# Folding a gate into two output weights on GpSimd, and turning the two-map outputs one unit later

## The chip, the cores and the metric

The kernel runs on one core of a Trainium2 chip. The metric is device time in microseconds (us) of one execution. The core's engines work side by side and in order, each from its own queue: TensorE (PE, matmuls, with PEld for its weight loads), VectorE (DVE), ScalarE (ACT), GpSimd (POOL), and SyncE (SP), which here only issues DMAs.

## The reference

A transformer block of two layers on 512 tokens of width 1024, in float32. Layer 0 mixes by eight heads of stick-breaking attention and eight of a sparse attention (an index picks 128 keys per query); layer 1 by eight heads of differential attention, the difference of two softmax maps ("two-map heads"). After each mixer comes a gated output product, a residual and a LayerNorm, then a gated feed-forward. What the change touches is the output product and the differential heads:

```python
h = x * (1.0 + sc_m) + sh_m
y = even_mixer(h, ...)          # or odd_mixer; each ends in  o @ w_out
x = layer_norm(ALPHA * x + (1.0 + g_m) * y, ln_mix_g[i], ln_mix_b[i])

# odd_mixer
p = softmax(where(causal, s, -inf)); a = p[:, :, 0] - lam * p[:, :, 1]
o = einsum('bhqs,bshe->bqhe', a, v)
o = rms_norm(o, subln_g) * (1.0 - lambda_init)
```

The gate `1 + g_m` is one number per output column, the same for all tokens. So `gate * (o @ w)` equals `o @ (w * gate)`.

## The kernel before, in words

**Products.** TensorE has no full float32 here: every operand is kept as a high and a low half of a narrower type, and `mm3` (L321 to L323) issues three matmuls for one product: high by high, high by low, low by high. Weights come from memory as 1 MB tiles `raw` (two buffers), loaded by SP. `split_w` (L288 to L300) makes the halves: ACT copies the high one (`wh`, L295), and the low one is a subtraction (`wl`, L299) on an engine taken in turn from a list, in the two-map stage DVE, DVE, GpSimd.

**Output products.** The 1024 rows of `w_out` are taken as two halves, k0 = 0 and k0 = 4. The first half is multiplied by `down_beside` (L577) while the other heads of the layer are still being made, beside them; the second half by `down_last` (L607). In `down_beside`, for each of two column halves h, `rows_w` (L553) loads four 128-row tiles, they are split, and for each of four token blocks b twelve matmuls sum into a PSUM tile `pd`. Then `partial` (L477) brings it into the residual `xa[b]`: it multiplies by the gate row `grow` into a tile `yt` (L479), and adds that to ALPHA times `xa` (L481), or to `xa` as it is (L483) where it is not the first half.

```python
        t = wd("yt")[:, :cs.stop - cs.start]
        dve.tensor_tensor(t, o, grow[:, cs], op=OP.mult)
        if first:
            dve.scalar_tensor_tensor(xa[b][:, cs], xa[b][:, cs], ALPHA, t, op0=OP.mult, op1=OP.add)
```

The gate rows are themselves made during the attention: `mod_side` sums them (`macc`, `ml` L221, `pm` L223) beside the stick-breaking heads.

**Two-map heads.** `diff_heads` (L1060 on) goes over 8 heads of 4 units (128 queries each). `pipeline` (L903) calls four stages at lags counted in units. `one` makes the two score tiles `zq` (L888), their mask and maximum (DVE, L880, `nm`), exponentials and the difference of the maps, `e`. `two`, L2 = 3 units later, transposes `e` on TensorE (`tp`, L895), and ACT copies that out of PSUM (`pt`, L898). `three`, 4 units behind `one`, multiplies by v into `o_df` (L1112); behind the head's last unit DVE, ACT and GpSimd make the norm: `oc` (L1116), `sq`, `st` (L1121 to L1125), a power on GpSimd (L1126, "the pow"), L1127, and `on` (L1129). `four`, 6 units behind, transposes `on` (L1139, into a tile `po`), and makes the halves `o_h` and `o_l` (L1144) that `down_beside` multiplies. Each head's q and k are split by ACT and GpSimd (L1072, tiles wh and wl 128x512).

**What sets the order.** `weave` mixes a main generator (heads) with a fill generator (projections, then `down_beside`) at a fixed ratio of planned costs; a scheduler then orders each engine's queue. Five buffers of 128x512 with the tag "wd" are shared by pt, oc, sq, on, of, the rope's rq and rt, and yt. PSUM has six banks "z" (zq, tp, o_df, the transposes' po) and two "pp" (projections, pd).

Of the kernel before, what the change touches and what calls it, by code (L numbers as in the profile page):

```python
# [12 lines left out]
OP = mybir.AluOpType  # L13
# [3 lines left out]
P = 128  # L17
S = 512
D = 1024
KT = D // P  # L20
EPS = 1e-5
ALPHA = 4.0 ** 0.25
# [9 lines left out]
TAIL2 = 1  # L32
# [4 lines left out]
L2 = 3  # L37
SEGS = [(0, 6), (6, 6), (12, 6), (18, 4)]
HALF = [slice(0, S), slice(S, 2 * S)]
# [8 lines left out]
def hybrid_kernel(ctx, tc, x, c, positions, w_mod, b_mod, w_in_even, w_out_even, w_in_odd,  # L48
# [3 lines left out]
    pe, act, dve, pool, sp = nc.tensor, nc.scalar, nc.vector, nc.gpsimd, nc.sync  # L52
# [8 lines left out]
    def acc(name="pp"):  # L61
        return ps.tile([P, S], F32, tag="pp", name=name, bufs=2)
# [4 lines left out]
    def wd(name, dt=F32):  # L67
        return T("wd", [P, S], dt, 5, name)
# [22 lines left out]
    xa = [cp.tile([P, D], F32, name=f"xa{b}") for b in range(4)]  # L91
# [94 lines left out]
    rows = {}  # L186
# [85 lines left out]
    def beside(main, side, every):  # L272

        for i, cost in enumerate(main):
            if i % every == every - 1:
                next(side, None)
            yield cost
# [197 lines left out]

    def partial(o, b, cs, grow, first):

        t = wd("yt")[:, :cs.stop - cs.start]
        dve.tensor_tensor(t, o, grow[:, cs], op=OP.mult)  # L479
        if first:  # L480
            dve.scalar_tensor_tensor(xa[b][:, cs], xa[b][:, cs], ALPHA, t, op0=OP.mult, op1=OP.add)  # L481
        else:
            dve.tensor_tensor(xa[b][:, cs], xa[b][:, cs], t, op=OP.add)  # L483
# [69 lines left out]
    def rows_w(w, k0, nk, h):  # L553

        t = raw()[:, :nk * S].rearrange("p (k m) -> p k m", m=S)
        sp.dma_start(t, w[P * k0:P * k0 + P * nk, S * h:S * h + S].rearrange("(k p) m -> p k m", p=P))
        return t
# [16 lines left out]
            for b in range(4):  # L574
                partial(os[b], b, HALF[h], grow, first)

    def down_beside(w, k0, ops, grow, first):  # L577

        for h in range(2):
            t = rows_w(w, k0, 4, h)  # L580
            ws = split_k(t[:, 0:2, :]) + split_k(t[:, 2:4, :])
            for b in range(4):
                bs = slice(P * b, P * b + P)
                o = acc("pd")
                for k in range(4):
                    mm3(o, (ops[k][0][:, bs], ops[k][1][:, bs]), ws[k], k == 0, k == 3)
                    yield 0.65
                partial(o, b, HALF[h], grow, first)

    def down_lead(w, k0, ops, lead=4):  # L590

# [78 lines left out]
    t = raw()  # L670
# [127 lines left out]
    oT = [None] * 8  # L798
# [104 lines left out]
    def pipeline(units, stages, tail):  # L903

        st = [{} for _ in units]
        last = max(lag for _, lag in stages)
        for t in range(len(units) + last):
            for f, lag in stages:
                u = t - lag
                if 0 <= u < len(units):  # L910
                    yield f(units[u], st[u])
            if t >= len(units) - 1:
                yield tail
# [74 lines left out]
    rest = beside(even_rest(), topk, 1)  # L988
    got_rows = []
# [6 lines left out]
    mods0 = mods_even()  # L996
    rest = beside(rest, mods0, 4)
# [3 lines left out]


    def even_fill(rest):
        yield from rest
        while not got_rows:
            next(mods0)
        yield from beside(down_beside(w_out_even[0], 0, oT[:4], rows[0, 2], True), mods0, 2)
        drain(mods0)
    rest = even_fill(rest)
    weave(dsa_heads(qd, kd), rest, DSA_FILL)  # L1010
# [51 lines left out]
    def diff_heads(qk):  # L1062
# [82 lines left out]
            oT[h] = (a, b)  # L1145
            return 0.43

        yield from pipeline([(h, i) for h in range(8) for i in range(4)], ((one, 0), (two, L2), (three, L2 + 1), (four, L2 + 3)), TAIL2)

    qk_od = [(r1("q_od"), r1("k_od")) for _ in range(8)]  # L1150

# [8 lines left out]
    oT = [None] * 8  # L1160
# [3 lines left out]
        next(rest)  # L1164
    def odd_fill():
        yield from rest
        while oT[3] is None:
            yield None
        yield from down_beside(w_out_odd[0], 0, oT[:4], rows[1, 2], True)
    rest2 = odd_fill()  # L1170
    low_on(dve, dve, pool)
    weave(diff_heads(qk_od), rest2, DIFF_FILL)
# [109 lines left out]
```

## Time and profile before

| | us |
|---|---|
| three runs | 1330.69, 1331.32, 1336.52 |
| median | 1331.32 |
| the profiled execution | 1333.38 |
| its span, first to last instruction | 1331.3 |
| mean granted clock of TensorE | 0.985 |

Stages by the trace: first products and the sparse heads' index until some 130 us; stick-breaking heads to 230; sparse heads with the first half of w_out_even beside them, 233 to 290; second half and LayerNorm to 340; feed-forward to 690; v of layer 1 to 750; two-map heads to 930, with the first half of w_out_odd beside them from about 880; second half and LayerNorm to 970; feed-forward to the end.

How to read it: the page gives each engine's busy share of the span; the table by stretches gives the same within a window, with the clock that was granted there (1.00 is full speed); the table of waits adds up an engine's idle time by what ended it; a timeline lists instructions with their start, their length, and in brackets the idle time before them. Names are the program's (out<-in). L-numbers are lines of the kernel before unless the text is about the change.

### The profile page before, as it was taken

The page shows a single profiled execution, that of the slowest core. Times are in us where ns is not written, and L with a number is a line of the kernel's source. Part 1 is how long each engine was busy: PE and PEld are TensorE (multiplying, and loading weights), DVE is VectorE, ACT ScalarE, POOL GpSimd, SP SyncE. Part 2 cuts the span into 40 slices and gives each one's busy share as a digit, 9 for nine tenths or more (in the row PEclk, how much of TensorE's full clock was granted, in tenths as well). Part 3 has the DMA queues.
Part 4 walks back from the last instruction along what each step waited for, and adds up shares of the span by engine and source line. Part 5 has one row for each costly group of instructions (what it writes and reads, how often), then busy time and mean ns, then how long its engine had stood idle before and what let it go on. Part 6 is the DMA issues. An engine that isn't in the chain of part 4 may idle for free.

```text
span 1331.3 us, 17597 instructions
## 1 busy us (share of the span) xinstructions
PE 1283.0 (96%) x6707; PEld 1017.8 (76%) x6707; DVE 885.8 (67%) x1605; ACT 498.8 (37%) x889; POOL 246.4 (19%) x173
## 2 busy tenths in 40 slices
PE   6999998999999999999999999898999999999995
PEld 5767676668888888888888866676888888888884
DVE  3789996987866665665694387787786335335358
ACT  2445544554432222222244356565443322322210
POOL 0103223001800000000017244443280000000004
PEclk9999989999999999999999999999999999999998
DMA  9953234342365555555423422215235223233211
GB/s 265 279 174 95 88 112 139 99 126 96 92 219 157 192 169 173 190 172 189 141 68 111 127 64 84 88 52 175 78 97 190 75 100 110 95 96 95 95 64 63
DMA packets 134388, 169.47 MB, mean 127 GB/s; under 512 B 7800, under 2 KB 89120, under 8 KB 134304
## 3 DMA queue, kind: packets, MB, share of 16 engines
q1 hardware_dynamic: 133568, 167.31, 39.9%
q8 instruction: 52, 0.85, 0.3%
q10 hardware_dynamic: 576, 1.02, 0.2%
q14 instruction: 32, 0.26, 0.1%
q0 software_dynamic: 160, 0.03, 0.0%
HBM read 159.95 MB, written 2.10 MB: 122 GB/s over the span
## 4 chain that ended last, share of the span: by engine, by line
PE 49%; issue 26%; DVE 13%; ACT 4%; DMA 3%; POOL 3%; SPq 1%; DVEq 0%; ACTq 0%; POOLq 0%
PE po L321 7%; PE po L322 7%; PE po L323 7%; PE pd L321 4%; PE pd L323 4%; PE pd L322 4%; DMA wm<-in_w_mod_dram 2%; PE pv L321 1%; PE pv L322 1%; PE pv L323 1%; DMA rt<-rq 1%; PE pf L322 1%; PE pf L323 1%; PE pf L321 1%; DVE yt L479 1%
## 5 line engine op out<-in xcount | busy, mean ns | idle before, releaser
L295 ACT ACTIVATE wh<-raw 128x1024 fp32r<-128x1024 f32 x174 | 183.8, 1065 | 499.8 <-PE po L322 268.6
L299 DVE TENSOR_TENSOR wl<-raw,wh 128x1024 fp32r<-128x1024 f32 x169 | 238.3, 1414 | 169.5 <-ACT wh L295 169.3
L321 PE MATMUL po<-hh,wh 128*128 128x512 f32 x848 | 340.9, 402 | 0.4 <-DVE sg L631 0.3
L323 PE MATMUL po<-hh,wl 128*128 128x512 f32 x848 | 333.4, 393 | 0.0
L322 PE MATMUL po<-hl,wh 128*128 128x512 f32 x848 | 333.3, 393 | 0.0
L321 PEld LDWEIGHTS po<-hh,wh 128*128 128x128 f32 x848 | 160.6, 189 | 40.0 <-issue 6.4
L323 PEld LDWEIGHTS po<-hh,wl 128*128 128x128 f32 x848 | 160.8, 190 | 34.1
L322 PEld LDWEIGHTS po<-hl,wh 128*128 128x128 f32 x848 | 160.9, 190 | 30.4
L502 POOL TENSOR_TENSOR lnv<-lnv,mhalf 128x1 f32<-128x1 f32 x16 | 11.6, 723 | 683.7 <-DVE lnv L500 683.5
L322 PE MATMUL pd<-wl,hid_h 128*128 128x512 f32 x352 | 137.2, 390 | 0.0
L323 PE MATMUL pd<-wh,hid_l 128*128 128x512 f32 x352 | 137.0, 389 | 0.0
L321 PE MATMUL pd<-wh,hid_h 128*128 128x512 f32 x352 | 137.0, 390 | 0.0
L212 DVE SCALAR_TENSOR_TENSOR macc<-wm,silu_c,macc 128x512 f32<-128x512 f32 x140 | 108.1, 775 | 6.8 <-DMA wm<-in_w_mod_dram 4.6
L631 DVE TENSOR_TENSOR sg<-sg,po 128x512 f32<-128x512 f32 x40 | 27.5, 686 | 118.3 <-PE po L323 118.3
L321 PEld LDWEIGHTS pd<-wh,hid_h 128*128 128x128 f32 x352 | 66.1, 188 | 14.1 <-issue 0.4
L322 PEld LDWEIGHTS pd<-wl,hid_h 128*128 128x128 f32 x352 | 66.1, 188 | 13.8 <-DVE wl L299 0.3
L323 PEld LDWEIGHTS pd<-wh,hid_l 128*128 128x128 f32 x352 | 66.1, 188 | 13.7
L479 DVE TENSOR_TENSOR yt<-pd,grow 128x512 f32<-128x512 f32 x96 | 64.1, 682 | 10.2 <-PE pd L323 10.1
L321 PE MATMUL pd<-wh,o_h 128*128 128x512 f32 x128 | 57.0, 445 | 0.0
L323 PE MATMUL pd<-wh,o_l 128*128 128x512 f32 x128 | 51.8, 405 | 0.0
L322 PE MATMUL pd<-wl,o_h 128*128 128x512 f32 x128 | 51.4, 401 | 0.3 <-DVE wl L299 0.3
L1094 ACT ACTIVATE e<-e,nm 128x128 f32<-128x128 f32 (+3 forms) x64 | 35.4, 555 | 36.8 <-DVE nm L1093 25.2
(276 smaller groups left out, 2021.4 us busy)
## 6 DMA issues: line engine op xcount, KB each, us to landing
wm<-in_w_mod_dram SPq DMA_DIRECT2D x56, 512.0 KB, 5.0
raw<-in_w_gate_dram SPq DMA_DIRECT2D x22, 1024.0 KB, 5.4
raw<-in_w_up_dram SPq DMA_DIRECT2D x22, 1024.0 KB, 5.4
wm<-in_w_mod_dram SPq DMA_DIRECT2D x80, 256.0 KB, 4.0
raw<-in_w_down_dram SPq DMA_DIRECT2D x16, 1024.0 KB, 5.1
raw<-in_w_in_odd_dram SPq DMA_DIRECT2D x12, 1024.0 KB, 5.2
raw<-in_w_in_even_dram SPq DMA_DIRECT2D x6, 1024.0 KB, 7.7
raw<-in_w_down_dram SPq DMA_DIRECT2D x12, 512.0 KB, 3.3
```

The source lines that it names most:

```text
L212: dve.scalar_tensor_tensor(a, t[:, k, :], silu_c[:, k0 + k:k0 + k + 1], a, op0=OP.mult, op1=OP.add)
L295: act.activation(oh, src, AF.Copy)
L299: e.tensor_tensor(ol, src, oh, op=OP.subtract)
L321: pe.matmul(o, lhsT=ah, rhs=bh, start=start, stop=False, skip_group_check=True)
L322: pe.matmul(o, lhsT=ah, rhs=bl, start=False, stop=False, skip_group_check=True)
L323: pe.matmul(o, lhsT=al, rhs=bh, start=False, stop=stop, skip_group_check=True)
L479: dve.tensor_tensor(t, o, grow[:, cs], op=OP.mult)
L502: norm_done["pow"] = pool.tensor_tensor(y, v[:, 1:2], mhalf[:, 0:1], op=OP.pow).ins
L631: dve.tensor_tensor(g, g, o, op=OP.mult)
L1094: act.activation(es[j], es[j], AF.Exp, scale=-1.0, bias=nm, accum_out=ss[:, j, i:i + 1])
```

## The change

`partial` gets a short form: with `grow` None it adds the PSUM tile straight to `xa`, one DVE operation (for a first half L481, now `xa<-xa,pd`) and no `yt`. Only `down_beside` uses it. In exchange a new function `gated_rows` loads the rows and multiplies them by the gate row in place, two GpSimd operations of 128x1024 (L589) for each of the four tiles, before they are split. The first tile is asked for earlier: in the even layer during the projections, once the gate row exists, in the odd layer before waiting for the fourth head's output; the second tile in the middle of the first one's products. In `diff_heads`, `three` stands 5 units behind `one` where it stood 4, and `four` 7 where it stood 6.

```diff
--- before.py
+++ after.py
@@ -475,6 +475,13 @@
 
     def partial(o, b, cs, grow, first):
 
+        if grow is None:
+            t = xa[b][:, cs]
+            if first:
+                dve.scalar_tensor_tensor(t, t, ALPHA, o, op0=OP.mult, op1=OP.add)
+            else:
+                dve.tensor_tensor(t, t, o, op=OP.add)
+            return
         t = wd("yt")[:, :cs.stop - cs.start]
         dve.tensor_tensor(t, o, grow[:, cs], op=OP.mult)
         if first:
@@ -574,18 +581,29 @@
             for b in range(4):
                 partial(os[b], b, HALF[h], grow, first)
 
-    def down_beside(w, k0, ops, grow, first):
-
+    def gated_rows(w, k0, h, gate):
+
+        t = rows_w(w, k0, 4, h)
+        for k in range(0, 4, 2):
+            v = t[:, k:k + 2, :]
+            pool.tensor_tensor(v, v, gate[:, HALF[h]].unsqueeze(1).to_broadcast([P, 2, S]), op=OP.mult)
+        return t
+
+    def down_beside(w, k0, ops, grow, first, ts=None):
+
+        first_t = ts.pop() if ts else gated_rows(w, k0, 0, grow)
         for h in range(2):
-            t = rows_w(w, k0, 4, h)
+            t = first_t if h == 0 else t1
             ws = split_k(t[:, 0:2, :]) + split_k(t[:, 2:4, :])
             for b in range(4):
                 bs = slice(P * b, P * b + P)
                 o = acc("pd")
+                if (h, b) == (0, 0):
+                    t1 = gated_rows(w, k0, 1, grow)
                 for k in range(4):
                     mm3(o, (ops[k][0][:, bs], ops[k][1][:, bs]), ws[k], k == 0, k == 3)
                     yield 0.65
-                partial(o, b, HALF[h], grow, first)
+                partial(o, b, HALF[h], None, first)
 
     def down_lead(w, k0, ops, lead=4):
 
@@ -1001,10 +1019,14 @@
 
 
     def even_fill(rest):
-        yield from rest
+        ts = []
+        for n, cost in enumerate(rest):
+            if n >= 4 * KT and got_rows and not ts:
+                ts.append(gated_rows(w_out_even[0], 0, 0, rows[0, 2]))
+            yield cost
         while not got_rows:
             next(mods0)
-        yield from beside(down_beside(w_out_even[0], 0, oT[:4], rows[0, 2], True), mods0, 2)
+        yield from beside(down_beside(w_out_even[0], 0, oT[:4], rows[0, 2], True, ts), mods0, 2)
         drain(mods0)
     rest = even_fill(rest)
     weave(dsa_heads(qd, kd), rest, DSA_FILL)
@@ -1145,7 +1167,7 @@
             oT[h] = (a, b)
             return 0.43
 
-        yield from pipeline([(h, i) for h in range(8) for i in range(4)], ((one, 0), (two, L2), (three, L2 + 1), (four, L2 + 3)), TAIL2)
+        yield from pipeline([(h, i) for h in range(8) for i in range(4)], ((one, 0), (two, L2), (three, L2 + 2), (four, L2 + 4)), TAIL2)
 
     qk_od = [(r1("q_od"), r1("k_od")) for _ in range(8)]
 
@@ -1164,9 +1186,10 @@
         next(rest)
     def odd_fill():
         yield from rest
+        ts = [gated_rows(w_out_odd[0], 0, 0, rows[1, 2])]
         while oT[3] is None:
             yield None
-        yield from down_beside(w_out_odd[0], 0, oT[:4], rows[1, 2], True)
+        yield from down_beside(w_out_odd[0], 0, oT[:4], rows[1, 2], True, ts)
     rest2 = odd_fill()
     low_on(dve, dve, pool)
     weave(diff_heads(qk_od), rest2, DIFF_FILL)
```

The diff shifts lines: by 7 behind `partial`, by 18 from the stick-breaking heads on, by 22 in the two-map heads (tp is L913, pt L916, o_df L1134, oc L1138, the pow L1148, on L1151, the transposes L1161, q and k splits L1094).

**TensorE, around the end of the second head.** Before (tp is of the next head's first unit, o_df x4 of this head's last):

```order
L895 MATMUL tp<-ct,e 128x128
L1112 MATMUL o_df<-v_od,pt 128x128 x4
L321 MATMUL po<-hh,wh 128x512
L322 MATMUL po<-hl,wh 128x512
L323 MATMUL po<-hh,wl 128x512
L321 MATMUL po<-hh,wh 128x512
L322 MATMUL po<-hl,wh 128x512
L323 MATMUL po<-hh,wl 128x512
L888 MATMUL zq<-wl,wh 128x128 x6
```

Now:

```order
L913 MATMUL tp<-ct,e 128x128 x2
L321 MATMUL po<-hh,wh 128x512
L322 MATMUL po<-hl,wh 128x512
L323 MATMUL po<-hh,wl 128x512
L1134 MATMUL o_df<-v_od,pt 128x128 x4
L321 MATMUL po<-hh,wh 128x512
L322 MATMUL po<-hl,wh 128x512
L323 MATMUL po<-hh,wl 128x512
L906 MATMUL zq<-wl,wh 128x256 x6
```

The products o_df of the head's last unit stood directly behind the first transposes of the next head. They now stand one unit later, behind the two transposes of its second unit.

**DVE, at one head's norm in the middle of the two-map heads.** Before (`e,nm<-zq` are the masks, 128x128 those of a head's first unit):

```order
L1095 RECIPROCAL rr<-ss 128x1
L1116 TENSOR_SCALAR oc<-o_df 128x512
L1096 TENSOR_SCALAR rr<-rr,ss,lam 128x1
L1097 SCALAR_TENSOR_TENSOR e<-e,rr 128x512
L1121 TENSOR_REDUCE st<-sq 128x4
L880 ISA e,nm<-zq,bias_c 128x128
L880 ISA nm 128x1
L1123 SCALAR_TENSOR_TENSOR st<-st 128x4
L1124 TENSOR_SCALAR st<-st 128x4
L1093 TENSOR_SCALAR nm<-nm 128x1
L880 ISA e,nm<-zq,bias_c 128x128
L880 ISA nm 128x1
```

Now (L898 are the masks, L1138 is oc):

```order
L1117 RECIPROCAL rr<-ss 128x1
L1118 TENSOR_SCALAR rr<-rr,ss,lam 128x1
L1119 SCALAR_TENSOR_TENSOR e<-e,rr 128x128
L1138 TENSOR_SCALAR oc<-o_df 128x512
L898 ISA e,nm<-zq,bias_c 128x256
L898 ISA nm 128x1
L898 ISA e,nm<-zq,bias_c 128x256
L898 ISA nm 128x1
L1115 TENSOR_SCALAR nm<-nm 128x1
L1117 RECIPROCAL rr<-ss 128x1
L1118 TENSOR_SCALAR rr<-rr,ss,lam 128x1
L1119 SCALAR_TENSOR_TENSOR e<-e,rr 128x256
```

The masks of the next head's first unit stood between the sum and the scaling of the norm; now they, and those of the second unit, stand ahead of the sum.

**GpSimd, heads 5 and 6 of the two-map stage.** Now (L1148 is the pow of a norm, L1166 o_l, L464 the rope):

```order
L589 TENSOR_TENSOR raw<-raw,grow 128x1024 x2
L464 TENSOR_TENSOR rq<-rq,cos_t 128x512
L1166 TENSOR_TENSOR o_l<-of,o_h 128x512
L1094 TENSOR_TENSOR wh<-q_od,wh 128x512
L1148 TENSOR_TENSOR st<-st,mhalf 128x4
L464 TENSOR_TENSOR rq<-rq,cos_t 128x512
L1166 TENSOR_TENSOR o_l<-of,o_h 128x512
L299 TENSOR_TENSOR wl<-raw,wh 128x1024
L1094 TENSOR_TENSOR wl<-k_od,wl 128x512
L464 TENSOR_TENSOR rq<-rq,cos_t 128x512
L589 TENSOR_TENSOR raw<-raw,grow 128x1024 x2
L1148 TENSOR_TENSOR st<-st,mhalf 128x4
```

Before, there was no L589, and the other rows followed one another in much the same turn. The first pair is ahead of a rope product and the Q split of head 6, the second directly ahead of a pow, that of head 4's norm. In the stick-breaking stage a pair stands between the first and the second lo (L854, before L836) of head 4, and another at the same place in head 6; SP's order is the same there. In the two-map stage the second load of w_out_odd stands two ropes (eight DMAs) later in SP's queue than before, directly ahead of the third load, and the last rope's DMAs stand behind both; each load waits for a buffer.

## Rows read from the trace of the kernel before

**Rows 1.** Page, part 1: busy time, share of the span and instructions of each engine.
```profile
PE 1283.0 (96%) x6707; PEld 1017.8 (76%) x6707; DVE 885.8 (67%) x1605; ACT 498.8 (37%) x889; POOL 246.4 (19%) x173
```

**Rows 2.** Table by stretches: us, engines' busy time, granted clock, DMA.
```profile
233.00:290.00 57.00, 56.46 (x387) 38.13 (x388) 51.63 (x160) 30.42 (x85) 5.15 (x4) 0.94 0.31 95
...
840.00:844.00 4.00, 4.00 (x15) 3.09 (x16) 2.61 (x17) 2.44 (x9) 1.01 (x1) 0.57 0.14 33
844.00:848.00 4.00, 4.00 (x25) 3.02 (x24) 1.82 (x6) 1.57 (x5) 1.29 (x1) 1.00 0.14 35
880.00:930.00 50.00, 46.05 (x259) 35.57 (x257) 39.99 (x108) 27.59 (x63) 19.32 (x12) 0.99 0.37 124
928.00:932.00 4.00, 3.81 (x13) 3.17 (x14) 1.23 (x2) 3.06 (x6) 1.29 (x1) 0.63 0.01 4
```

**Rows 3.** Table of TensorE's waits, 740 to 980 us: total us, times, longest.
```profile
PE o_df L1112 <- ACT pt L898: 4.2, 4, 1.8
PE po L1139 <- DVE on L1129: 4.0, 3, 2.6
PE zq L888 <- DVE nm L880: 3.5, 3, 2.1
```

**Rows 4.** Timeline, PE, three places: start, length, idle before and releaser in brackets.
```profile
163.91 0.50 PE L223 MATMUL pm<-ml,cst_r 128*128 128x512 f32 x1 [0.55 <-DVE ml L221]
...
840.00 0.74 PE L888 MATMUL zq<-wl,wh 64*128 64x256 f32 x5 [2.08 <-DVE nm L880]
...
928.19 0.63 PE L1139 MATMUL po<-ct,on 128*128 128x128 f32 x4 [2.60 <-DVE on L1129]
```

**Rows 5.** Groups by line and shape, DVE: count | busy us, mean ns | idle before.
```profile
L299 DVE TENSOR_TENSOR wl<-raw,wh 128x1024 fp32r<-128x1024 f32 x169 | 238.3, 1414 | 169.5 <-ACT wh L295 169.3
...
L479 DVE TENSOR_TENSOR yt<-pd,grow 128x512 f32<-128x512 f32 x96 | 64.1, 682 | 10.2 <-PE pd L323 10.1
...
L631 DVE TENSOR_TENSOR sg<-sg,po 128x512 f32<-128x512 f32 x40 | 27.5, 686 | 118.3 <-PE po L323 118.3
...
L481 DVE SCALAR_TENSOR_TENSOR xa<-xa,yt 128x512 f32<-128x512 f32 x32 | 23.6, 759 | 0.2
```

**Rows 6.** Groups by line and shape, POOL.
```profile
L541 POOL TENSOR_TENSOR xa<-xa,lnb 128x1024 f32<-128x1024 f32 x12 | 37.8, 3173 | 0.0
L540 POOL TENSOR_TENSOR xa<-xa,lng 128x1024 f32<-128x1024 f32 x12 | 34.9, 2931 | 0.0
...
L299 POOL TENSOR_TENSOR wl<-raw,wh 128x1024 fp32r<-128x1024 f32 x5 | 12.1, 2423 | 7.2 <-ACT wh L295 4.0 <-issue 3.3
```

**Rows 7.** Timeline, POOL: a lo of head 4, the pow of head 4, the LayerNorm.
```profile
161.05 1.29 POOL L836 TENSOR_TENSOR lo<-l,hi 128x512 fp32r<-128x512 f32 x1 [1.70 <-DVE hi L835]
...
880.09 1.01 POOL L1126 TENSOR_TENSOR st<-st,mhalf 128x4 f32<-128x4 f32 x1 [3.18 <-PE zq L888]
...
969.96 5.76 POOL L540 TENSOR_TENSOR xa<-xa,lng 128x1024 f32<-128x1024 f32 x2
```

**Rows 8.** Timeline, DVE, four places.
```profile
162.88 0.98 DVE L221 TENSOR_TENSOR ml<-macc,mh 128x512 fp32r<-128x512 f32 x1
...
881.13 0.16 DVE L1127 TENSOR_TENSOR st<-st 128x4 f32<-128x4 f32 x1 [1.05 <-POOL st L1126]
...
921.73 1.78 DVE L481 SCALAR_TENSOR_TENSOR xa<-xa,yt 128x512 f32<-128x512 f32 x1
...
970.17 13.31 DVE L299 TENSOR_TENSOR wl<-raw,wh 128x1024 fp32r<-128x1024 f32 x4 [1.44 <-ACT wh L295]
```

**Rows 9.** Timeline, SP: loads of rows of the two output weights.
```profile
153.62 0.38 SPq L556 DMA_DIRECT2D raw<-in_w_out_even_dram  x1
...
855.74 0.37 SPq L556 DMA_DIRECT2D raw<-in_w_out_odd_dram  x1
...
875.84 0.37 SPq L556 DMA_DIRECT2D raw<-in_w_out_odd_dram  x1
```

**Rows 10.** DMA issues: count, KB each, median us to landing.
```profile
raw<-in_w_out_odd_dram SPq DMA_DIRECT2D x4, 1024.0 KB, 5.7
```


## Prediction, on record before the change was run

> **What bounds the kernel now.** I read the busy shares first: TensorE works 1283.0 of 1331.3 us, 96% [rows 1], so only time that its queue loses can be won, and whatever makes it wait is paid in full. Next comes the table by stretches, for the two places where the change works [rows 2]. In the DSA heads (233 to 290 us), where the first half of w_out_even is multiplied, TensorE is busy 56.46 of 57 us: taking DVE work away there gains at most half a microsecond. In the last two-map heads (880 to 930 us), where the first half of w_out_odd is multiplied, it is busy 46.05 of 50, and DVE 39.99. The table of waits for 740 to 980 us says what TensorE waits for in the two-map stage [rows 3]: 4.2 us in four waits of the second product o_df for ACT's copy pt; 4.0 in three waits of the four transposes po for DVE's normalised rows on; 3.5 in three waits of the scores zq, whose bank is free only once DVE has read it (nm). That is 11.7 us. Last I looked at what follows a wait. After the one of 2.08 us at 840.00 [rows 4] the granted clock is 0.57 over 840 to 844 us, and 1.00 in the next four [rows 2], about the lower of its two levels (1.2 against 2.4 GHz): 4 x 0.43 = 1.7 us of work lost. After the 2.60 us at 928.19 [rows 4] it is 0.63 in 928 to 932 [rows 2]: 4 x 0.37 = 1.5 us. So up to 11.7 + 3.2 = 14.9 us are to be had in this stage.
>
> **Part 1: the gate folded into the weights, on DVE.** Sixteen blocks (8 in each product) lose their yt and keep one operation. Before, a block cost 682 + 759 ns; now it is one op of a PSUM tile and an SBUF tile. Its nearest row is the 686 ns addition of a PSUM tile at L631, its upper bound the 759 ns of the old second op [rows 5]. DVE saves 682 to 755 ns a block, 10.9 to 12.1 us in all. I count the even half of it as nothing, since TensorE is full there [rows 2]; if TensorE were not, it would be worth 0.5 us. The odd half (about 6 us out of DVE's 39.99) shortens waits counted in part 3 and is not counted again.
>
> **Part 2: the same fold, on GpSimd.** Eight operations are added, each 128x1024 with two SBUF inputs. The rows of that shape on GpSimd are 2423, 2931 and 3173 ns [rows 6]; I take 2.93, so 23.4 us (19.4 to 25.4), and a pair is 5.9 us. GpSimd is idle most of the time, so the cost is in what queues behind a pair, and in DVE. At 969.96 us GpSimd runs two of its 128x1024 multiplications in 5.76 us, with more such work behind them [rows 7], and the four splits wl on DVE beside them take 13.31 us [rows 8], 3.33 each against a mean of 1.41 over the run [rows 5]: a DVE op with two SBUF inputs is held for about the length of a GpSimd op.
> The Trainium skill (GPSIMD Engine Reference, 1. Specifications) says the same, that GpSimd shares its SBUF interfaces with VectorE and contends with instructions that have two SBUF inputs; these rows agree, and by it the fold would lengthen DVE's queue rather than relieve it.
>
> *Even, first pair.* The load goes out at 153.62 [rows 9] and, at the 5.7 us that the other product's loads take [rows 10], lands at 159.3. In the built order the pair stands between the first and the second lo of head 4, so it runs at about 159.4 to 165.3 (the first lo is done by then) and pushes the second lo from 161.05 [rows 7] to 165.3. I find no wait of TensorE on lo in this stage, and count that as nothing; without that cover it would cost the same 4 us. But DVE's ml, 0.98 us at 162.88 [rows 8], has two SBUF inputs, and TensorE already waits 0.55 us for it at 163.91 [rows 4]. Held by one gate operation it ends 2.4 us later, held by both 4.9 us; by none, it costs 0. I take 1.5, as the ml may just as well fall between the two. The second pair lies in head 6 with no such wait nearby: 0.
>
> *Odd, first pair.* It stands behind the K split of head 5 and ahead of a rope multiply and the Q split of head 6. A score of head 6 needs that split. From 0, if the ropes' lead covers it, to a whole pair, 5.9; I take 2.0: TensorE has about a dozen projection products to do before it needs those scores, an estimated 2 to 3 us (259 matmuls take 46.05 us in 880 to 930 [rows 2], 0.18 each, the wide ones more), and the rope's DMAs leave some room too.
>
> *Odd, second pair.* Its load waits for a buffer that GpSimd's own split frees, and the pair stands directly ahead of the pow of head 4 (before at 880.09 [rows 7]). DVE's next operation, at 881.13, already waits 1.05 us for that pow [rows 8] with masks and partials queued behind it in order, and TensorE needs those masks to get score banks back. 0 if the rows land well ahead of the pow; 5.9 if the pair starts when the pow is due. I take 2.0, nearer the low end, because the built order gives TensorE a dozen projection products between chain and transposes. In SP's queue the third load and the last rope's DMAs stand behind this load, so its wait can hold head 7's k as well; that is the same lateness seen from another queue, with a head of some 20 us in between, and I add nothing for it beyond the 5.9.
>
> Each pair also holds one of the two raw buffers 5.9 us longer and the next load into it starts that much later. Loads land in 5.7 us (median) [rows 10] and go out 20 us apart (855.74, 875.84 [rows 9]): 0. With less lead it would be another 5.9.
>
> **Part 3: the later turn.** o_df now comes one unit (about 5 us: 32 units in the 160 us from 770 to 930) later, behind its neighbour's transposes; the copy pt gets that much more time, so the 4.2 us of waits on it [rows 3] should go. I take 3.2, not all, since there are only five wd buffers: pt now holds one for two units, in which about six others are asked for. For zq the order puts the masks of a head's first unit ahead of the previous head's chain on DVE, where they stood inside it; I take half of 3.5 + 1.7 with the clock, 2.6. The transposes po keep the same distance from the chain; only the last one gains: its oc stood behind a 1.78 us xa, held beside GpSimd [rows 8], and the yt ahead of it, 0.68 [rows 5], which now goes. I take 2.3 of 4.0 + 1.5.
>
> **The sum.** Gains 3.2 + 2.6 + 2.3 = 8.1 (0 to 14.9); losses 1.5 + 2.0 + 2.0 = 5.5 (0 to 4.9 + 5.9 + 5.9 = 16.7). Net -2.6 from the profiled execution's 1333.38 us, 1330.8. That execution lies 2.06 above the median of 1331.32, so I forecast **1328.7 us**.
>
> **Rivals.** *A, the lag takes nearly all the waits and GpSimd's pairs are covered.* For it: every wait in [rows 3] is for something late by less than a unit, 2.6 us at most. Against: three engines are busy over half of the time there. 14.9 - 1.5 gives 13.4, less a microsecond for new short waits: about 1319 us.
> *B, the two odd pairs decide (the slow side).* If the second pair is still running when the pow of head 4 is due, GpSimd's queue holds the pow, DVE stands in order behind it, and TensorE loses its score banks; the first pair does the same to head 6's Q split. It decides from the point where a pair ends later than its successor was due by more than those 2 to 3 us of queued products. 5.9 + 5.9, and 1.7 for the clock as at 840 us, 1.5 in the even part, less 8.1: +6.9, about 1338 us. For it: DVE waits for GpSimd's pow even now. Against: GpSimd has 50 - 19.32 us free in 880 to 930 [rows 2].
> The Trainium skill (Perfetto Trace Analysis, Optimizing Scalar/DVE Operations) warns that moving work between GpSimd and DVE may not help as they share a read port; B is how that would look here.
> *C, the five wd buffers eat the lag.* ACT's pt, sq and the chain then wait for o_df to free a buffer, and the waits move instead of going. Gains drop to 2.3, losses stay 5.5: +3.2, about 1334.5 us.
>
> **Chances.** Forecast 0.43 (about 1324 to 1333), A 0.24, C 0.20, B 0.13. No change means within 0.5%, 6.7 us, about what a measurement of this kernel can tell. Faster by more: A, and 0.07 of the forecast's low edge, 0.31. Slower by more (over 1338): half of B and 0.07 of C's and the forecast's upper tail, 0.14. The same: 0.55. The range of 8 in 10 leaves out the far end of A and that of B: 1319 to 1338.
>
> **What would show it.** Right: o_df waits for pt under 1 us in all; DVE's busy time down by 5 to 12 us; GpSimd's up by 20 to 25; pm's wait for ml up by one to two us; single waits of TensorE for zq or po around the two odd pairs, at most 3 us each; the clock at 1.00 around the head 2 to 3 border. B would show as a pow of head 4 that starts right at the end of a gate pair, with DVE and then TensorE idle behind it. C would show as pt or sq on ACT released by o_df. If the stage's waits come to under 2 us, A holds. If TensorE waits where the profile of before has no wait at all, in the DSA heads above all, my costing of the even part is wrong.

## The result and the profile after

The change made the kernel slower: 1353.2 us, median of six runs (1351.96 to 1355.17), against 1333.34 for the kernel before beside it (1329.93 to 1338.2). The ratio is 1.0156, with a 95% interval of 1.0135 to 1.0176. The forecast was 1328.7, the range 1319 to 1338. The profiled execution took 1352.99 us, with a span of 1350.9.

The page's first part of the kernel after (busy us, share of the span, instructions), to be held against [rows 1]:

```profile
PE 1286.3 (95%) x6707; PEld 1020.5 (76%) x6707; DVE 893.7 (66%) x1589; ACT 498.9 (37%) x889; POOL 266.0 (20%) x181
```

TensorE does 3.3 us more work in the same 6707 matmuls. GpSimd has 19.6 us more, as counted. DVE has 7.9 us *more*, though sixteen operations are gone.

Where do the 20 us lie? The last power operation on GpSimd of each of the four LayerNorms is a landmark that both traces have. Before, they stand at 327.26, 699.42, 957.73 and 1321.24 us; after, at 329.50, 701.52, 977.72 and 1340.78. So the kernel is 2.2 us late after layer 0's mixer, 2.1 after its feed-forward, 20.0 after layer 1's mixer and 19.5 at the last one. 17.9 of the 20 us are lost between the second and the third landmark, the two-map heads with the products about them; it is called **the stage** from here on, and its length is given for each run. The early 2.2 us can't be laid to a cause: in the experiments' profiles that share the early code of the kernel before, the first landmark stands anywhere from 324.63 to 335.00, in those with the even fold from 325.72 to 330.75. A stage's length scatters too: one kernel profiled twice (experiments 4 and 18) gave 258.4 and 260.8, so 2 to 3 us between two stages are no evidence.

The table by stretches for the stage, of the kernel before (columns: sum; busy us of PE, PEld, DVE, ACT, POOL with instructions; granted clock; DMA share; GB/s):

```profile
699.42:957.73 258.31, 245.22 (x1289) 191.84 (x1288) 180.89 (x448) 129.92 (x292) 111.03 (x74) 0.99 0.30 92
```

The same view of the kernel after, and under it three short stretches that are spoken of below:

```profile
701.52:977.72 276.20, 250.47 (x1289) 195.03 (x1288) 188.98 (x440) 129.62 (x292) 119.46 (x78) 0.96 0.28 86
...
833.00:839.00 6.00, 5.70 (x22) 3.90 (x23) 3.14 (x12) 4.00 (x9) 0.37 (x1) 0.64 0.20 46
857.00:861.00 4.00, 4.00 (x14) 2.41 (x13) 2.25 (x6) 1.79 (x6) 0.00 (x0) 0.50 0.56 164
888.00:892.00 4.00, 4.00 (x12) 2.67 (x12) 1.94 (x4) 0.00 (x0) 3.14 (x2) 0.51 0.92 301
```

The stage is 17.9 us longer. TensorE is busy 5.25 us longer in the same 1289 matmuls, at a mean granted clock of 0.96 in place of 0.99; it idles 276.20 - 250.47 = 25.7 us, where it idled 13.1. DVE has eight operations fewer and 8.1 us more busy time.

What TensorE waits for, 760 to 990 us of the kernel after (total us, times, longest), answering to [rows 3]:

```profile
PE po L1161 <- DVE nm L1115: 9.6, 2, 5.3
PE zq L906 <- POOL wl L1094: 3.4, 1, 3.4
PE po L323 <- POOL wl L299: 3.3, 1, 3.3
PE po L1161 <- DVE on L1151: 2.9, 3, 1.4
PE zq L906 <- DVE nm L898: 2.5, 3, 1.3
```

Four readings. The waits of o_df for pt, 4.2 us before, are gone. The waits of the transposes po for the norm's DVE chain, 4.0 before, are now 9.6 + 2.9 = 12.5. The scores zq wait 2.5 for nm (3.5 before). And two waits on a low half made by GpSimd (wl) are new, 3.4 and 3.3. In the timeline of TensorE (start, length, then idle before and releaser in brackets) the first row answers to pm in [rows 4], 0.55 there:

```profile
166.15 0.79 PE L223 MATMUL pm<-ml,cst_r 128*128 128x512 f32 x1 [4.02 <-DVE ml L221]
...
833.30 1.12 PE L1161 MATMUL po<-ct,on 128*128 128x128 f32 x4 [5.29 <-DVE nm L1115]
...
856.48 1.12 PE L1161 MATMUL po<-ct,on 128*128 128x128 f32 x4 [4.30 <-DVE nm L1115]
...
887.29 0.80 PE L323 MATMUL po<-hh,wl 128*128 128x512 f32 x1 [3.30 <-POOL wl L299]
...
915.20 0.44 PE L906 MATMUL zq<-wl,wh 64*128 64x128 f32 x4 [3.42 <-POOL wl L1094]
```

The two long ones are at the borders of heads, 833 and 856 us, at a norm chain each. After the one of 5.29 us the granted clock is 0.64 over 833 to 839 us; it is 0.50 over 857 to 861, behind the one of 4.30, and 0.51 over 888 to 892, behind the one of 3.30: at or near the lower level, as after the waits of [rows 4].

How the chain of one head, the second, became so late is seen on three engines. First DVE in the kernel before, from oc to on:

```profile
817.64 0.69 DVE L1116 TENSOR_SCALAR oc<-o_df 128x512 f32<-128x512 f32 x1
...
821.99 1.24 DVE L1127 TENSOR_TENSOR st<-st 128x4 f32<-128x4 f32 x1 [1.05 <-POOL st L1126]
823.26 0.69 DVE L1129 TENSOR_TENSOR on<-o_df,st 128x512 f32<-128x512 f32 x1
```

The same chain on DVE after:

```profile
822.27 0.68 DVE L1138 TENSOR_SCALAR oc<-o_df 128x512 f32<-128x512 f32 x1
...
825.51 0.68 DVE L1143 TENSOR_REDUCE st<-sq 128x4 f32<-128x512 f32 x1
...
826.12 0.69 DVE L463 TENSOR_TENSOR rt<-rt,sin_t 128x512 f32<-128x512 f32 x1
826.73 1.24 DVE L1145 SCALAR_TENSOR_TENSOR st<-st 128x4 f32<-128x4 f32 x1
...
827.99 0.69 DVE L465 TENSOR_TENSOR k_od<-rq,rt 128x512 f32<-128x512 f32 x1
...
829.88 2.29 DVE L1149 TENSOR_TENSOR st<-st 128x4 f32<-128x4 f32 x1 [0.65 <-POOL st L1148]
...
832.56 0.68 DVE L1151 TENSOR_TENSOR on<-o_df,st 128x512 f32<-128x512 f32 x1
```

ACT of the kernel after, the two operations ahead of st:

```profile
823.68 0.51 ACT L1116 ACTIVATE e<-e,nm 128x256 f32<-128x256 f32 x1 [1.75 <-DVE nm L898]
...
824.67 0.62 ACT L1140 ACTIVATE sq<-oc 128x512 f32<-128x512 f32 x1
```

GpSimd of the kernel after, beside the chain:

```profile
826.15 1.80 POOL L464 TENSOR_TENSOR rq<-rq,cos_t 128x512 f32<-128x512 f32 x1 [4.65 <-DMA rt<-rq]
...
829.80 2.34 POOL L299 TENSOR_TENSOR wl<-raw,wh 128x1024 fp32r<-128x1024 f32 x1
```

Before, this chain takes 6.3 us from the start of oc to the end of on; now 833.24 - 822.27 = 11.0. Three things lengthen it. First, oc ends at 822.95, but sq starts at 824.67, where before it started 0.4 us behind the end of oc: in the built order it now stands 19 matmuls behind oc (4 before), and ACT does the next head's exponentials ahead of it. That is 1.3 us. Secondly, tiny DVE operations on 128x4 are held beside GpSimd: the one at 826.73 takes 1.24 us beside rq (0.26 before), the one at 829.88 takes 2.29 us beside a wl of 2.34. The latter was held before too, at 821.99, but for 1.24 us only; together this is 2.0 us. Thirdly, DVE's rope operations rt and k_od, which came behind the chain, now stand inside it; they are most of the 1.4 us that are left. The transposes that wait for on start at 833.30.

The eight chains took 6.8, 6.3, 5.1, 7.3, 6.2, 5.0, 4.6 and 4.6 us before, and 6.2, 11.0, 10.2, 5.6, 8.4, 6.0, 4.6 and 4.6 after. So it is the second and third head that became late, those of the two long waits. In the built order their sq stands 19 and 21 matmuls behind oc, that of the other six 3 to 9; before it was 3 or 4 in all eight.

### The profile page after: what moved, and what is told of

Read it like the earlier page. It is cut to its first block, busy times and chain, and to the rows that moved or that the text cites. A ratio compares the mean times of both kernels' runs of the same rounds, so it can differ in the third digit from the quotient of the medians.

```text
span 1350.9 us, 17585 instructions
## 1 busy us (share of the span) xinstructions
PE 1286.3 (95%) x6707; PEld 1020.5 (76%) x6707; DVE 893.7 (66%) x1589; ACT 498.9 (37%) x889; POOL 266.0 (20%) x181
## 4 chain that ended last, share of the span: by engine, by line
PE 49%; issue 26%; DVE 11%; POOL 4%; DMA 4%; ACT 3%; SPq 2%; DVEq 0%; POOLq 0%; ACTq 0%
PE po L321 7%; PE po L323 7%; PE po L322 7%; PE pd L321 4%; PE pd L323 4%; PE pd L322 4%; DMA wm<-in_w_mod_dram 2%; PE pv L321 1%; PE pv L322 1%; PE pv L323 1%; PE pf L322 1%; PE pf L323 1%; PE pf L321 1%; DMA rt<-rq 1%; PE zq L906 1%
## 5 line engine op out<-in xcount | busy, mean ns | idle before, releaser
L486 DVE TENSOR_TENSOR yt<-pd,grow 128x512 f32<-128x512 f32 x80 | 53.1, 682 | 10.4 <-PE pd L323 10.3
```

## The experiments

A run's line gives its median, the ratio to the kernel before beside it with its interval, and the stage in its profile (258.3 us in the kernel before). "Lag" is the change's pair of lags in the kernel before, "the fold" all the rest of the change.

**1. The change cut in two, and the fold cut in two.** Experiment 1 has the lag alone:

```diff
-  (three, L2 + 1), (four, L2 + 3)
+  (three, L2 + 2), (four, L2 + 4)
```

> Before with the two lags alone (o_df 5 and the transposes 7 units behind the scores), no fold. Theory 1, the later turn is the main loss: the transposes wait 4 to 5 us each for the normalised rows in heads 2 and 3 as in the change, and the kernel is 8 to 14 us slower than before. Rival 2, the gate pairs on GpSimd are the loss: this kernel is between 4 us faster and 2 us slower. Rival 3, only the two together are slow: within 4 us of before.

Experiment 2 is the changed kernel with that line put back.

> The change with the old lags (4 and 6 units), both folds kept. Theory 1: 4 to 9 us slower than before, of it 2.2 from the even part (ml held beside the first gate pair) and the rest from the odd pairs. Rival 2: 14 to 20 us slower. Rival 3: within 4 us of before, but for the 2.2 of the even part.

In experiments 3 and 4 only one output product has the fold, the even and the odd one; the other calls the old form:

```diff
-        yield from down_beside(w_out_odd[0], 0, oT[:4], rows[1, 2], True, ts)
+        yield from down_plain(w_out_odd[0], 0, oT[:4], rows[1, 2], True)
```

> Before with the even fold alone. All theories: about 2 us slower (1 to 4): the one wait of pm for ml of 4 us, as in the trace of the change, the clock's fall behind it, and 1 to 2 us given back in the sparse heads. If it is within 0.5 us of before, what is lost at ml is made up later.

> Before with the odd fold alone, old lags. Theory 1: 2 to 6 us slower, from waits around the two gate pairs. Rival 2: 12 to 17 us slower. Rival 3: within 3 us of before. If it is faster, DVE's shorter queue is worth more than the pairs cost.

| | median us | ratio | stage us |
|---|---|---|---|
| 1, lag | 1348.39 | 1.0094 (1.0061 to 1.0126) | 273.2 |
| 2, fold | 1336.29 | 1.0003 (0.9981 to 1.0025) | 260.0 |
| 3, even fold | 1333.91 | 1.0002 (0.9981 to 1.0023) | 259.1 |
| 4, odd fold | 1331.10 | 0.9969 (0.9949 to 0.9990) | 258.4 |

The lag is what costs: 0.0094 x 1334.67 = 12.5 us alone, with 14.9 us in the stage, on unchanged instructions. The fold alone costs nothing that can be measured. The two don't quite add up to the change: by the ratios (0.0156 - 0.0094 - 0.0003) x 1333.34 = 7.9 us are left over, by the stages 17.9 - 14.9 - 1.7 = 1.3. The intervals of the change (from 1.0135) and of the lag (to 1.0126) just miss each other, so what the two cost together, beyond each alone, stays open. The lag's waits in experiment 1 are nearly those of the change, down to the two on wl (TensorE's waits, 740 to 1000 us):

```profile
PE po L1139 <- DVE nm L1093: 9.6, 2, 5.3
PE po L1139 <- DVE on L1129: 5.0, 3, 2.5
PE po L323 <- POOL wl L299: 3.3, 1, 3.3
PE zq L888 <- POOL wl L1072: 2.8, 1, 2.8
```

So the wl waits don't come from the gate pairs, since this kernel has none. The odd fold alone seemed to gain 0.3%; experiment 18 ran it again.

> The odd fold alone, as e4, again. If the fold pays: 1 to 4 us faster than before, with an interval that leaves out 1. By e4's own trace, whose two-map stage takes 258.35 us against 258.31 before, it is within 1 us, and e4's gain was chance.

It took 1334.42 us, ratio 0.9997 (0.9979 to 1.0015), stage 260.8: no gain.

**2. Which half of the lag.** Experiment 7 delays only the transposes (`L2 + 1`, `L2 + 4`), experiment 12 only o_df (`L2 + 2`, `L2 + 3`).

> Only the transposes one unit later (7 behind the scores), o_df at its old place (4 behind). Theory 1a: pt holds no buffer longer, the chain stays short; the waits of the transposes for on go to about 0, those of o_df for pt stay (4.2 us): 2 to 6 us faster than before. Rival: on and of hold buffers longer instead, and ACT's copies are late: 2 to 8 us slower.

> Only o_df one unit later (5 behind the scores), the transposes at their old place (6). Since the transposes alone one unit later (e7) cost nothing, all theories but one have this at 10 to 20 us slower than before: pt's buffers are held as in e1, and the chain has a unit less. If it is within 5 us of before, the loss of e1 needs both lags, and the buffers are not its cause.

Experiment 7: 1334.97 us, 1.0009 (0.9989 to 1.0029), stage 262.3. Experiment 12: 1351.99 us, 1.0129 (1.0088 to 1.0170), stage 276.2. Later transposes alone cost nothing that can be measured (nor did they gain the 2 to 6 us of theory 1a), so the loss comes with the later o_df. Experiment 12 is not a clean half, though: it leaves the chain one unit less before the transposes, and most of its loss stands there (TensorE's waits, 740 to 1000 us):

```profile
PE po L1139 <- DVE on L1129: 16.9, 6, 4.6
PE po L1139 <- DVE rr L1095: 6.6, 2, 4.0
```

**3. Buffers.** pt is made at L2 and used by o_df. With the lag it holds one of five shared buffers for two units, so that sq may find none free. Experiment 5 is the lag with sq written over oc, so that it asks for none; 6 is its control on the kernel before; 8 the whole change with it:

```diff
-                sq = wd("sq")
+                sq = oc
```

> The lags alone, as in e1, but the square is written over oc and takes no wd buffer of its own. Theory 1a, the buffers: with the lag, pt holds its buffers for two units, sq finds none free and is put far behind oc, and the norm's chain is late for the transposes. Then this kernel has no wait of the transposes over 2.5 us (5.3 and 4.3 in e1), and stands between 6 us faster than before and 4 us slower. Rival 1b, the masks in the middle of the chain and GpSimd's splits that hold DVE's small operations: waits of 3 us and more for the normalised rows stay, 6 us and more slower than before.

> Control: the kernel before, with the square written over oc. Both theories: within 3 us of before, since sq stood right behind oc there anyway.

> The change with the square written over oc. Theory 1a: most of the 20 us goes; within 6 us of before. Rival 1b: 10 us and more slower than before. If it stands in between, the gate pairs and the lag cost something together that neither costs alone.

Experiments 9 (lag), 10 (control on the kernel before) and 11 (whole change) leave sq alone and take pt out of the shared ring, into three buffers that are otherwise empty in this stage:

```diff
-            st["t"] = transposed(st["e"], i, act)
+            st["t"] = transposed(st["e"], i, act, T("wm", [P, S], F32, 3, "pt"))
```

> The lags alone, with pt taken out of the five wd buffers (it gets three buffers of another tag, wm, that the gate rows' sums use in other stages). Theory 1a, the buffers: pt, sq and the rope's tiles all waited for a wd buffer; now no wait of TensorE in the two-map stage is over 2.7 us, and the kernel is between 6 us faster and 4 us slower than before. Rival 1c, the later turn itself: with o_df and its norm a unit later, DVE's masks, the rope and the splits come in an order that is late for TensorE whatever the buffers; 8 us and more slower than before.

> Control: the kernel before with pt in its own three buffers. Theory 1a: within 4 us of before, at best 4 us faster, as the ropes' tiles find a buffer sooner. Rival 1c: within 3 us of before.

> The change with pt in its own three buffers. Theory 1a: within 6 us of before. Rival 1c: 12 to 20 us slower than before, as the change is.

| | median us | ratio | stage us |
|---|---|---|---|
| 5, lag, sq over oc | 1344.44 | 1.0087 (1.0058 to 1.0116) | 269.1 |
| 6, control | 1332.14 | 0.9996 (0.9971 to 1.0021) | 259.6 |
| 8, change, sq over oc | 1345.57 | 1.0096 (1.0067 to 1.0124) | 268.4 |
| 9, lag, pt apart | 1343.89 | 1.0068 (1.0043 to 1.0093) | 268.5 |
| 10, control | 1340.47 | 1.0045 (1.0022 to 1.0067) | 264.5 |
| 11, change, pt apart | 1341.63 | 1.0057 (1.0035 to 1.0079) | 268.1 |

With sq over oc the two long waits at the borders are gone, but others have come (TensorE's waits in experiment 5, 740 to 1000 us):

```profile
PE po L1139 <- DVE on L1129: 4.9, 3, 2.5
PE zq L888 <- DVE nm L880: 3.8, 3, 2.6
PE zq L888 <- POOL wl L1072: 2.7, 1, 2.7
PE po L323 <- POOL wl L299: 2.7, 1, 2.7
PE tp L895 <- DVE nm L880: 2.6, 2, 1.8
```

Either edit brings the two long chains back to their old length. In the built order sq stands 3 to 7 matmuls behind oc in experiments 5 and 9, and the chains of the second and third head take 6.4 and 6.1 us in experiment 5, 5.5 and 7.3 in experiment 9. So the shared buffers are what put sq far behind oc and made these two chains long, and the transposes wait 4.9 and 4.2 us for on, about as long as in the kernel before (4.0).

The time doesn't come back with it. On the whole change both edits gain clear of noise, (1.0156 - 1.0096) x 1333.34 = 8.0 us in experiment 8 and 13.2 in experiment 11. On the lag alone the ratios of experiments 5 and 9 overlap with that of experiment 1; by the stages the lag costs 9.5 us against its control with sq over oc, where it cost 14.9, and 3.9 with pt apart. But that last control is itself 6 us slower than the kernel before, more than either theory allowed, so it doesn't prove that the ring made the other 11: a stage that has lost its time already may hide the lag's. Against the kernel before, experiments 5 and 9 are still 11.6 and 9.1 us slower by their ratios (10.8 and 10.1 in the stage), where theory 1a allowed 4; experiment 8, 12.8 us slower, is on the side of rival 1b, and 11, with 7.6, on neither side. Sharing of buffers is a part of the loss, about 5 to 11 us by the two controls' stages and 8 to 13 by the ratios of the whole change, and not more can be said. Both edits together were not tried.

**4. Fewer projections ahead.** In the built order, the lag leaves 14 matmuls with the high halves of the projections' weights to be done behind the first score of the seventh head, where the kernel before leaves 4. Experiment 13 gives the lag two more projection products of lead, 14 adds sq over oc, 15 is the whole change with both.

```diff
-    for _ in range(2 * ODD0 * KT):
+    for _ in range(2 * ODD0 * KT + 2):
```

> The lags alone (e1), and the projections get a lead of two products before the two-map heads begin, which brings their count before each head back to that of the kernel before. Theory 2, a late fill: the waits of TensorE for the splits wl of weights, q and k (6.7 us in e1) go, and the kernel is 4 to 8 us faster than e1, so 5 to 9 us slower than before; the waits for the normalised rows stay. Theory 1a alone: as e1, 11 to 15 us slower than before.

> Lags, lead of two products, and the square over oc. If late fill and buffers are the whole loss: within 4 us of before, or faster. If something else of the later turn costs time: 6 to 10 us slower than before, as e5 and e9.

> The change with the lead of two products and the square over oc. If late fill and buffers are the whole loss: within 6 us of before. Otherwise 8 to 13 us slower, as e8.

Medians 1348.30, 1346.51 and 1353.14 us; ratios 1.0115 (1.0076 to 1.0153), 1.0107 (1.0064 to 1.0151) and 1.0154 (1.0113 to 1.0194); stages 273.2, 272.9 and 278.4. Nothing is won, and with sq over oc it is no better than without the lead. The lead does bring the count back to 4, but it also moves sq, to 23, 22 and 16 matmuls behind oc in the second to fourth head, so experiment 13 alone is no clean test; in experiment 14, where sq stands 3 to 7 behind, the loss is there all the same, and larger than the 6 to 10 us of its rival. This theory falls.

**5. GpSimd beside DVE.** DVE was busy 12.5 us longer in the lag's stage than in the kernel before, in the same instructions. The stage of experiment 1, to be held against that of the kernel before:

```profile
700.83:974.04 273.21, 249.90 (x1289) 194.94 (x1288) 193.36 (x448) 129.44 (x292) 110.86 (x73) 0.96 0.28 87
```

Does the new order pay more for GpSimd's company? Experiments 16 (lag) and 17 (the kernel before) leave out GpSimd's 16 multiplies by the cosine in layer 1's ropes, and nothing else; the order of all other instructions on TensorE, DVE, ACT and SP is that of experiment 1 and of the kernel before.

```diff
-            pool.tensor_tensor(q, q, cos_t, op=OP.mult)
+            if cos:
+                pool.tensor_tensor(q, q, cos_t, op=OP.mult)
```

> The lags alone, and layer 1's ropes leave out their GpSimd multiply by cos (16 operations, 23 us of GpSimd); the order on TensorE, DVE, ACT and SP is that of e1. Theory 3, the shared port: DVE's busy time in the stage falls by 5 us and more, and the kernel is 6 us and more faster than e1. Rival 4, the order as such: DVE's operations wait for one another whoever holds them; less than 4 us faster than e1.

> Control: the kernel before without the same 16 multiplies. Theory 3: 2 to 5 us faster than before, so the gap to e16 shrinks from some 13 us to 8 and less. Rival 4: within 4 us of before, and the gap to e16 stays at 10 us and more.

Medians 1337.98 and 1326.54 us, ratios 1.0042 (1.0020 to 1.0065) and 0.9952 (0.9925 to 0.9979). The stage by the table of stretches, experiment 16 and then 17:

```profile
696.91:962.74 265.83, 248.43 (x1289) 194.97 (x1288) 184.14 (x448) 130.19 (x292) 88.05 (x57) 0.96 0.29 90
```

```profile
697.11:947.47 250.36, 241.57 (x1289) 189.66 (x1288) 171.79 (x448) 129.69 (x292) 88.61 (x58) 1.00 0.30 95
```

Both orders gain alike: the stage 7.4 us (from 273.2) and 8.0 (from 258.3), DVE's busy time 9.2 and 9.1 us, for 23 us of GpSimd work left out. The gap between them is 15.5 us, where it was 14.9; theory 3 had it shrink. By its ratio experiment 16 is 6.9 us faster than experiment 1, which alone would have spoken for theory 3; the control, 6.4 us faster than the kernel before, decides against it. So the company of these multiplies is a tax that both orders pay, and not the lag's loss.

But they are only 23 of GpSimd's 111 us in the stage, and without them DVE is still busy 12.4 us longer in the lag's order. A count in the traces says where: every DVE operation that took over 150 ns more than the median of its kind (operation, tiles and shape, over all traces) ran beside a GpSimd operation, and in the stage these excesses sum to 22.8 us in the kernel before and 33.6 with the lag, to 14.3 and 24.5 without the multiplies. So the lag's order holds DVE 10 to 11 us more, beside the rest of GpSimd's work. What that costs TensorE was not tested. It can hardly be the whole loss: experiment 16 has an excess near that of the kernel before, 24.5 and 22.8 us, and a stage 7.5 us longer.

At the head borders the lag without the multiplies still waits (TensorE, 740 to 1000 us):

```profile
PE po L1140 <- DVE nm L1094: 4.8, 2, 2.9
PE po L1140 <- DVE on L1130: 4.3, 2, 2.5
PE po L323 <- POOL wl L299: 3.3, 1, 3.3
PE zq L889 <- POOL wl L1073: 2.8, 1, 2.8
```

The waits of 5.3 us have become 2.9 at most, those on wl are as they were.

No version that computes everything was shown to be faster than both kernels.

## Why the prediction was wrong

**The bound** was read rightly: TensorE sets the time, and what it waits for, with the lower clock behind it, is paid. Of the stage's 17.9 us, 12.6 are idle time and 5.25 slower matmuls.

**The step that failed is part 3.** It says "the copy pt gets that much more time, so the 4.2 us of waits on it [rows 3] should go", and they went. But it took the rest of the order as it was: "The transposes po keep the same distance from the chain". In units they do; the chain itself went from 6.3 to 11.0 us in the second head and from 5.1 to 10.2 in the third, and TensorE waited 12.5 us in all for the chains in place of 4.0. For a gain of 8.1 us (0 to 14.9) the lag alone gave a loss of 12.5 us by its ratio and of 14.9 in the stage. Nothing in my bounds let part 3 lose; the lower end should have been below zero. I gave sq and the norm no new place, though the built order had sq 19 and 21 matmuls behind oc in those two heads.

**Rival C** named the mechanism in part (pt holds a shared buffer for two units, sq waits), at a chance of 0.20. It did not show as I wrote, as sq waiting for o_df on ACT; the built order itself puts sq behind the exponentials. Its price, +3.2, only took the gain away, as if a moved wait could be no longer than the old one. Experiments 5 and 9 show that the buffers made the two chains long, and 8 and 11 that this is worth 8 to 13 us of the whole change. What carries the rest stays open. The projections' lead isn't it, and the cosine multiplies beside DVE aren't. That the lag's order holds DVE 10 to 11 us more beside GpSimd's other work was not tested as a cause, and neither was what the lag and the fold cost together.

**Part 2, the gate on GpSimd.** Its length was nearly right: 20.2 us in all, 2.545 us each, near the low one of [rows 6] and not the 2.93 that I took. GpSimd's group by line in the kernel after (instructions, busy us and mean ns of one, idle before):

```profile
L589 POOL TENSOR_TENSOR raw<-raw,grow 128x1024 f32<-128x1024 f32 x8 | 20.2, 2545 | 8.9 <-DVE rr L1117 7.6 <-DMA raw<-in_w_out_odd_dram 1.3
```

*Even.* The pair starts at 159.40 as worked out, and the ml beside it is late. GpSimd, then DVE, of the kernel after:

```profile
159.40 4.88 POOL L589 TENSOR_TENSOR raw<-raw,grow 128x1024 f32<-128x1024 f32 x2
...
892.48 5.18 POOL L589 TENSOR_TENSOR raw<-raw,grow 128x1024 f32<-128x1024 f32 x2 [1.33 <-DMA raw<-in_w_out_odd_dram]
...
900.55 1.01 POOL L1148 TENSOR_TENSOR st<-st,mhalf 128x4 f32<-128x4 f32 x1 [2.89 <-DVE st L1147]
```

```profile
160.13 1.95 DVE L853 CAST hi<-l 128x512 fp32r<-128x512 f32 x1
...
164.82 1.27 DVE L221 TENSOR_TENSOR ml<-macc,mh 128x512 fp32r<-128x512 f32 x1
...
892.87 2.55 DVE L463 TENSOR_TENSOR rt<-rt,sin_t 128x512 f32<-128x512 f32 x1
...
896.00 2.21 DVE L465 TENSOR_TENSOR q_od<-rq,rt 128x512 f32<-128x512 f32 x1
```

hi<-l, a conversion, takes 1.95 us beside the pair (0.44 in the mean of the kernel before), ml starts 1.9 us later than before and takes 1.27; pm waits 4.02 us, 3.5 more, within the bounds of 0 to 4.9 and above the 1.5 taken. Yet experiments 2 and 3 show ratios of 1.000 with the even fold: in experiment 2 this wait is 3.68 us, and one of the scores for a k (kd_l) has fallen from 4.4 to 0.7. By these rows a wait only moved.

*Odd.* In experiment 4, where the lag is absent, GpSimd ran thus:

```profile
857.88 5.15 POOL L589 TENSOR_TENSOR raw<-raw,grow 128x1024 f32<-128x1024 f32 x2 [0.24 <-DMA raw<-in_w_out_odd_dram]
...
868.02 4.73 POOL L589 TENSOR_TENSOR raw<-raw,grow 128x1024 f32<-128x1024 f32 x2
...
885.78 1.01 POOL L1157 TENSOR_TENSOR st<-st,mhalf 128x4 f32<-128x4 f32 x1 [3.18 <-PE zq L919]
```

Both pairs are done 13 us or more ahead of the pow of head 4 (885.78), which waits for something else. So the 2.0 + 2.0 for the odd pairs were nothing, and with the even part the loss of 5.5 was nothing that can be measured: ratio 1.0003. In the changed kernel the pow of 900.55 comes 2.9 us after the pair's end and waits for DVE's st. **Rival B**'s queue did not happen; what the pair does there is hold DVE's rt to 2.55 us and q_od to 2.21.

**Part 1, DVE.** The single operation took 678 ns, just under the 686 to 759 that I took (DVE's group by line in the kernel after):

```profile
L481 DVE SCALAR_TENSOR_TENSOR xa<-xa,pd 128x512 f32<-128x512 f32 x16 | 10.9, 678 | 1.9 <-PE pd L323 1.8
```

But the 10.9 to 12.1 us hardly show in DVE's total: 884.3 us in experiment 2 against 885.8 before. Most of the rest came back in held operations: over the whole kernel, DVE's excesses over the medians (counted as under 5 above, and all of them beside a GpSimd operation) sum to 72.1 us in the kernel before and 80.2 in experiment 2, 8.1 more. The four rows of DVE above are instances, beside the pairs.

The Trainium skill (Perfetto Trace Analysis, Optimizing Scalar/DVE Operations) warns that moving work between GpSimd and DVE may not help; this trace agrees, with 1.5 us less DVE for 18 us more GpSimd in experiment 2.

**The rows that should have shown it** were the right ones: o_df<-pt gone, DVE down by 5 to 12 (it was up 7.9), GpSimd up by 20 to 25 (19.6), pm up by one to two (3.5), no wait over 3 us (5.3, 4.3, 3.4, 3.3), the clock at 1.00 at the head 2 to 3 border (0.50, now at 857 to 861 us). I had looked for new waits only around the odd pairs; that they would grow at po ahead of any pair (at 833 and 856 us, the first odd pair being at 863) was on no list of mine.

## What to carry to other kernels

A stage that is moved one turn later keeps every operand of that turn alive one turn longer: count the buffers of the ring it draws on, look up in the built order who stands behind them, and let the lower bound of the gain fall below zero. Removing the wait that a table names is not a gain until the work queued behind it has been followed to its own next wait: here 4.2 us of waits went, and those at the place next to it grew from 4.0 to 12.5. Before moving work from DVE to GpSimd, price the DVE operations that will run beside it, the smallest ones too.

## What was not expected of the hardware

GpSimd's company costs even the smallest DVE operations: one on 128x4 took 2.29 us beside a GpSimd subtraction of 2.34, and a conversion with one SBUF input 1.95 us in place of 0.44. Priced by experiments 16 and 17, 23 us of GpSimd multiplies cost DVE 9 us of busy time and the kernel 7.4 to 8.0 us of the stage, though GpSimd was busy under half of it; in the latter price the ropes' own waits for these multiplies are included.
The Trainium skill (GPSIMD Engine Reference, 1. Specifications) says that GpSimd shares its SBUF interfaces with VectorE; the rows agree, and add that in these places the small operations were held as long as large ones.
